# The second pass of differential attention's scores over 128 rows instead of 64, with the queries' rounded half beside zeros

## The chip, the cores and the metric

The kernel runs on one core of a Trainium2 chip. The metric is device time in microseconds (us) of one execution, as the median of several runs. The engines are TensorE (PE in the profile, with its weight loads shown apart as PEld), VectorE (DVE), ScalarE (ACT), GpSimd (POOL) and SyncE (SP, which here only issues transfers).

## The reference

One layer works on 1024 latent tokens of width 1024 and 256 context tokens. An input projection feeds two groups of heads side by side, differential attention and a gated delta rule; then come the output projection, a router with 16 experts that each take 128 tokens, and a norm. The change lies in the attention, which has four heads of two softmax halves of depth 64:

```python
def diff_attn(q, k, v, lam):
    ...
    qb = jnp.moveaxis((q * DA_D ** -0.5).reshape(B, nblk, Q_BLOCK, DA_HEADS, 2, DA_D), 1, 0)

    def block(qi):
        s = jnp.einsum('bqhid,bkhid->bhiqk', qi, k).astype(jnp.float32)
        p = jax.nn.softmax(s, axis=-1)
        a = (p[:, :, 0] - lam * p[:, :, 1]).astype(v.dtype)
        return jnp.einsum('bhqk,bkhe->bqhe', a, v)
```

The scores `s` of a block of 128 queries and one half have 1280 columns: 1024 latent and 256 context keys.

## The kernel before, in words

Float32 products of width 256 and more run as float32r passes. Each operand is split exactly into a rounded part, hi, and its rest, lo, and the product is hi·hi + lo·hi + hi·lo. Projections take three passes of depth 128 (`mm3`, L169 to L174). The scores have depth 64, so two of the three fit into one pass of depth 128. `_head` (L969) loads, for a head's half s, the tile `QS` with the queries' hi in rows 64s to 64s+63 and their lo in the other 64 rows, the tile `KH` with the keys' hi twice, and, once for both halves, `KL` with the keys' lo (half 0 in rows 0 to 63, half 1 in rows 64 to 127).

`scores` (L1023) computes one half s for a tile t of 128 queries: three column blocks of 512, 512 and 256, each with two matmuls into the same PSUM columns. The first (L1027) is `QS` by `KH` over 128 rows. The second (L1028) is the queries' hi, the 64 rows of `QS` that hold it, by the matching 64 rows of `KL`. We call these six matmuls a scores group. Then VectorE takes the negated maximum `mx` (L1030) of the 1280 columns and ScalarE the exponential `pt` with its sum (L1033). There is one PSUM buffer `sp` for the scores, so the next group waits for that exponential. `combine` joins the two halves on VectorE (L1038 to L1041), `values` transposes the result (`ptr`, L1049), copies it (`aT`, L1051) and multiplies it by the values (`po`, L1055). There are 4 heads by 8 tiles by 2 halves, so 64 groups.

In the same stage the delta rule runs beside it (`_delta`). `levels` inverts the chunks' matrices with TensorE, VectorE, ScalarE and GpSimd in turn (tiles `X`, `lm`, `LTm`, `QF`, `QTr`, `U`, `W`). `scan` walks the chunks (`psc`, `u`, `S`), `outputs` gives `O`, and `finish` (L912) norms it and multiplies it by a gate. `finish` runs twice a head, for the inner and the outer chunks: it loads the gate into the tile `gT` (L919), multiplies in place (L938), and stores `gT` to `ot_dram` (L940). For the last head it splits parts of `gT` for the output projection instead, and one part of the inner `gT` is read by `_mixed` when the first tokens of that projection are prepared.

Each engine runs its instructions in one order, which a scheduler sets when the program is built, from priorities and its own idea of durations. An engine that waits holds up whatever stands behind. `K.after` (L119) is a copy of one column on GpSimd that holds a load back.

Of the kernel before, what the change touches and what calls it, by code (L numbers as in the profile page):

```python
"""Hybrid diffusion layer: differential attention and a gated delta rule side by side, then an
expert-choice mixture of experts, on one core.

float32 products of width 256 and more run as three float32r passes over operands that are split
exactly into a rounded part and its rest (h*h + l*h + h*l); narrower ones run in float32.
"""
# [22 lines left out]
P = 128  # L29
# [9 lines left out]
H = 4  # L39
# [15 lines left out]
GT, UB, SB = 2, 4, 4  # L55
# [21 lines left out]
# the tokens that the scans finish first come first  # L77
# [31 lines left out]
class _K:  # L109
# [7 lines left out]
    def after(self, dst, src):  # L117
        """A load to dst waits until src is there."""
        self.nc.gpsimd.tensor_copy(dst, src)  # L119

    def slot(self, kind, i=None, name=None, dt=F32):
        """A buffer of the queries' or keys' size; in turn, those first that the last head's projections leave first."""
        if i is None:
            order = (0, 1) if kind == "KL" else (0, 2, 1)
            i = order[self.turn[kind] % len(order)]
            self.turn[kind] += 1
        return self.qk.tile([P, L if kind == "QS" else LT], dt, name=name or kind, tag=f"{kind}{i}")
# [4 lines left out]
    def xT(self, kt, t, n):  # L132
        """The two parts of x^T for tiles t to t + n of a group."""
# [11 lines left out]
    def rsqrt_steps(self, pool, x, n, np_=P, tag=""):  # L145
        """1/sqrt(x) for positive x [np_, n]: three Newton steps from the bit estimate."""
# [22 lines left out]
    def mm3(self, out, ah, al, bh, bl, start, stop):  # L169
        """out (+)= a.T @ b in float32, from the split operands."""  # L170
# [10 lines left out]
def _decays(K, pg, ps):  # L181
    """Decays and betas of the delta rule: [token, direction, chunk, head]."""
# [55 lines left out]
def _prep(K, pg, ps, h, kvq):  # L238
    """Norms and decays of a head's chunks, their matrices and the inverses of the 16 x 16 diagonal blocks.

    With k = r k~ (k~ before its l2 norm), c = beta r^2, N = (k~ k~^T) * decay, a chunk of 128 tokens is
        u' = (I + N c)^-1 (v / r - e^G k~ S),   S' = e^Gl S + k~^T (c e^(Gl-G) u'),
        o  = r_q (e^G q~ S + ((q~ k~^T) * decay) c u').
    Both directions share a matrix: below the diagonal the forward one, above it the backward one.
    """
# [29 lines left out]
    # queries with the decay from their chunk's start, one set per direction  # L275
# [59 lines left out]
    # a 16 x 16 block per partition, by substitution  # L335
# [11 lines left out]
    def both(t, fwd, bwd, rows, cols):  # L347
        """A part of both directions' blocks, from an element of each on."""
# [3 lines left out]
    for j in range(15):  # L352
        # forward: rows after j gain their multiple of row j; backward: rows before 15 - j
# [16 lines left out]
def _inproj(K, banks):  # L370
    """Modulation, x^T and the input projection."""
# [7 lines left out]
    with tc.tile_pool(name="p1v", bufs=1, reuse_waits="tile") as pv, \  # L379
# [21 lines left out]
        # v of the attention and a, b of the delta rule, tokens on partitions  # L401
# [15 lines left out]
    # the rest, channels on partitions  # L417
# [109 lines left out]
def _modulation(K, pe, ps, psm):  # L527
    """Shift and scale of both token sets, channels on partitions; loads the first tokens on the way."""
# [23 lines left out]
    # silu(c), silu(c_ctx)  # L552
# [10 lines left out]
    for kt in range(KT):  # L563
# [4 lines left out]
        # of the last tile the scales in float32 at once, the shifts from split parts  # L568
# [26 lines left out]
def _tokens(K, pe, ps, xts, late):  # L595
    """x^T, modulated and split."""
# [31 lines left out]
def _row_vectors(K, pool, ps):  # L628
    """Gate 1, shift 2, scale 2 and gate 2 as rows in DRAM."""
# [29 lines left out]
def _mix(K, prep, left):  # L659
    """Differential attention and the delta rule's scans, side by side."""  # L660
# [3 lines left out]
    with tc.tile_pool(name="g", bufs=1, side="right", reuse_waits="tile") as pg, \  # L664
# [29 lines left out]
        # the first tokens of the output projection, in the buffers that the attention leaves  # L694
# [13 lines left out]
def _mixed(K, t, ol, oh, lo):  # L708
    """The parts of a tile's transposed mix."""
# [12 lines left out]
def _weights(K, pw):  # L722
    """The parts of most of w_out, in the buffers that the last head's scan leaves."""
# [14 lines left out]
    # what the attention's last head leaves  # L738
# [8 lines left out]
    # what is left of them takes the parts of the last head's mix  # L747
# [4 lines left out]
def _weight(K, k, hi, lo, raw):  # L752
    """The parts of a tile of w_out, its columns scaled by the gate."""
# [10 lines left out]
def _delta(K, pg, pw, gps, ps):  # L764
    """Inverses from the 16 x 16 blocks up, T <- T - T (off-diagonal block) T, and the scans of both directions."""
# [27 lines left out]
    def levels(h, st, c0, n):  # L793
        """Doubles the blocks up to the chunk, then W and U of both directions."""
# [50 lines left out]
    def all_levels(h, st):  # L845
        """The chunks' groups in interleaved streams."""
# [4 lines left out]
    # the context's chunks come first  # L851
# [14 lines left out]
    def scan(h, st, step):  # L866
        """One chunk of each direction."""
# [27 lines left out]
    def outputs(st, step):  # L895
        """Both directions' outputs of the last two steps, chunks ascending."""
# [15 lines left out]
    def finish(h, st, inner):  # L912
        """Gated norm of the inner or the outer chunks; they go to the transposed mix."""
# [55 lines left out]
def _head(K, h):  # L969
    """Queries' parts stacked; the keys' rounded parts twice, their rests once: passes of depth 128 and 64."""  # L970
# [19 lines left out]
def _attention(K, pa, ps):  # L990
    """Latent queries over latent and context keys; the two softmax halves of a head in turn."""
# [9 lines left out]
    # the first tiles lie where the projection ends last: these are needed later than queries and keys  # L1001
# [20 lines left out]

    def scores(st, t, s):  # L1023
        sp = ps.tile([P, 1536], F32, name="sp")
        qs = st["QS"][s][:, t * P:(t + 1) * P]
        for k0, k1 in ((0, 512), (512, 1024), (1024, 1280)):
            nc.tensor.matmul(sp[:, k0:k1], qs, st["KH"][s][:, k0:k1], start=True, stop=False)  # L1027
            nc.tensor.matmul(sp[:, k0:k1], qs[64 * s:64 * s + 64], st["KL"][64 * s:64 * s + 64, k0:k1], start=False, stop=True)  # L1028
# [637 lines left out]
```

## Time and profile before

| | us |
|---|---|
| median of 3 runs | 1759.38 (1756.13 to 1769.11) |
| span of the profiled execution, first to last instruction | 1753.3 |
| PE busy | 1596.4 (91%) |
| DVE busy | 1315.1 (75%) |
| ACT busy | 916.2 (52%) |
| POOL busy | 609.9 (35%) |

The profiled execution is told by its span alone; no other time of its own is given. The median of the runs lies 6.1 us above the span. The stage in which attention and the delta rule share the core runs from about 505 to 955 us, the output projection and the router follow, and the experts take the rest from about 1130 us on. A matmul's duration in the profile includes its way through the array, so two neighbours overlap; the distance between their starts tells what one costs.

### The profile page before, as it was taken

The page shows a single profiled execution, that of the slowest core. Times are in us where ns is not written, and L with a number is a line of the kernel's source. Part 1 is how long each engine was busy: PE and PEld are TensorE (multiplying, and loading weights), DVE is VectorE, ACT ScalarE, POOL GpSimd, SP SyncE. Part 2 cuts the span into 40 slices and gives each one's busy share as a digit, 9 for nine tenths or more (in the row PEclk, how much of TensorE's full clock was granted, in tenths as well). Part 3 has the DMA queues.
Part 4 walks back from the last instruction along what each step waited for, and adds up shares of the span by engine and source line. Part 5 has one row for each costly group of instructions (what it writes and reads, how often), then busy time and mean ns, then how long its engine had stood idle before and what let it go on. Part 6 is the DMA issues. An engine that isn't in the chain of part 4 may idle for free.

```text
span 1753.3 us, 24640 instructions
## 1 busy us (share of the span) xinstructions
PE 1596.4 (91%) x8793; PEld 1303.7 (74%) x8793; DVE 1315.1 (75%) x2110; ACT 916.2 (52%) x1514; POOL 609.9 (35%) x489
## 2 busy tenths in 40 slices
PE   6999899899979999999999998399999999999990
PEld 2897678788857878787787787278888877777780
DVE  6657845678667776667777744789999989989894
ACT  6521125434324545455465232287777777777773
POOL 3013321332244662371630122434565334441012
PEclk9999899999989999999999999599999999999995
DMA  7478852443564042412212484799999999999915
GB/s 268 154 250 249 246 169 92 155 128 118 162 183 114 24 103 91 109 48 74 85 54 100 143 307 167 265 359 358 399 385 398 399 384 353 357 360 375 369 37 216
DMA packets 170846, 377.17 MB, mean 215 GB/s; under 512 B 32542, under 2 KB 82140, under 8 KB 169572
## 3 DMA queue, kind: packets, MB, share of 16 engines
q1 hardware_dynamic: 131874, 315.22, 49.5%
q0 software_dynamic: 11664, 43.52, 8.3%
q10 hardware_dynamic: 27186, 16.86, 3.8%
q8 instruction: 69, 1.13, 0.3%
q14 instruction: 53, 0.43, 0.1%
HBM read 315.60 MB, written 55.76 MB: 212 GB/s over the span
## 4 chain that ended last, share of the span: by engine, by line
PE 65%; DVE 6%; DMA 5%; POOL 3%; ACT 3%; issue 2%; SPq 0%; ACTq 0%; POOLq 0%; DVEq 0%
PE sp L1028 4%; PE pgu L172 3%; PE po L1055 3%; PE sp L1027 3%; PE pgu L173 3%; PE pgu L174 3%; PE pgv L172 3%; PE pgv L174 3%; PE pgv L173 3%; PE py L173 3%; PE py L172 3%; PE py L174 3%; PE ptr L1049 2%; PE pp L172 2%; PE pp L173 2%
## 5 line engine op out<-in xcount | busy, mean ns | idle before, releaser
L1461 DVE TENSOR_TENSOR wlo<-raw,whi 128x1024 fp32r<-128x1024 f32 x376 | 453.3, 1241 | 40.8 <-ACT whi L1460 31.6
L1460 ACT ACTIVATE whi<-raw 128x1024 fp32r<-128x1024 f32 x384 | 399.1, 1059 | 134.0 <-PE pgu L173 53.5
L1412 POOL TENSOR_SCALAR onehot<-fcst,slot 128x128 bf16<-128x128 f32 x96 | 156.9, 2027 | 42.9 <-PE pls L1415 22.5
L173 PE MATMUL pl<-XH,wl 128*128 128x512 f32 x384 | 152.9, 398 | 3.7 <-DVE wl L178 3.7
L172 PE MATMUL pl<-XH,wh 128*128 128x512 f32 x384 | 153.2, 399 | 0.9 <-DVE ab L413 0.9
L174 PE MATMUL pl<-XL,wh 128*128 128x512 f32 x384 | 153.1, 399 | 0.0
L1030 DVE TENSOR_REDUCE mx<-sp 128x1 f32<-128x1280 f32 x64 | 95.2, 1487 | 54.5 <-PE sp L1028 54.1
L1526 POOL DMA_INDIRECT acc_dram<-y,idx x15 | 36.1, 2409 | 279.6 <-DVE y L1525 265.6
L172 PE MATMUL pgu<-whi,xTh 128*128 128x512 f32 x256 | 102.1, 399 | 18.1 <-ACT hid L1505 18.1
L1033 ACT ACTIVATE pt<-sp,mx 128x1280 f32<-128x1280 f32 x64 | 84.8, 1325 | 57.4 <-DVE mx L1030 54.1
L174 PE MATMUL pgu<-wlo,xTh 128*128 128x512 f32 x256 | 101.8, 398 | 0.0
L172 PE MATMUL pgv<-whi,xTh 128*128 128x512 f32 x256 | 101.7, 397 | 0.0
L173 PE MATMUL pgu<-whi,xTl 128*128 128x512 f32 x256 | 100.8, 394 | 0.0
L174 PE MATMUL pgv<-wlo,xTh 128*128 128x512 f32 x256 | 100.4, 392 | 0.0
L1027 PE MATMUL sp<-KH,QS 128*128 128x512 f32 (+1 forms) x192 | 89.3, 465 | 12.0 <-ACT pt L1033 6.8
L173 PE MATMUL pgv<-whi,xTl 128*128 128x512 f32 x256 | 99.7, 390 | 0.0
L174 PE MATMUL py<-wlo,hTh 128*128 128x512 f32 x240 | 94.6, 394 | 0.7 <-POOL wlo L1461 0.7
L172 PE MATMUL py<-whi,hTh 128*128 128x512 f32 x240 | 93.8, 391 | 0.0
L173 PE MATMUL py<-whi,hTl 128*128 128x512 f32 x240 | 93.6, 390 | 0.0
L1028 PE MATMUL sp<-KL,QS 64*128 64x512 f32 (+1 forms) x192 | 89.6, 467 | 0.0
L1055 PE MATMUL po<-V,aT 128*128 128x128 f32 x640 | 88.7, 277 | 0.0
L172 PEld LDWEIGHTS pl<-XH,wh 128*128 128x128 f32 x384 | 73.2, 191 | 20.3 <-issue 5.2
(540 smaller groups left out, 4008.1 us busy)
## 6 DMA issues: line engine op xcount, KB each, us to landing
raw<-w_gate SPq DMA_DIRECT2D x64, 1024.0 KB
raw<-w_up SPq DMA_DIRECT2D x64, 1024.0 KB
raw<-w_down SPq DMA_DIRECT2D x64, 1024.0 KB
rwm<-w_mod POOLq DMA_DIRECT2D x32, 512.0 KB, 6.3
wr<-w_in ACTq DMA_DIRECT2D x24, 512.0 KB
wm<-w_mod SPq DMA_DIRECT2D x8, 1024.0 KB
KH<-qk_dram SPq DMA_DIRECT2D x16, 320.0 KB
xt<-x SPq DMA_DIRECT2D x8, 512.0 KB
```

Source lines behind the costliest of these rows:

```text
L172: nc.tensor.matmul(out, ah, bh, start=start, stop=False)
L173: nc.tensor.matmul(out, al, bh, start=False, stop=False)
L174: nc.tensor.matmul(out, ah, bl, start=False, stop=stop)
L1027: nc.tensor.matmul(sp[:, k0:k1], qs, st["KH"][s][:, k0:k1], start=True, stop=False)
L1028: nc.tensor.matmul(sp[:, k0:k1], qs[64 * s:64 * s + 64], st["KL"][64 * s:64 * s + 64, k0:k1], start=False, stop=True)
L1030: nc.vector.tensor_reduce(mx, sp[:, :LT], axis=AX.X, op=ALU.max, negate=True)
L1033: nc.scalar.activation(pt, sp[:, :LT], AF.Exp, bias=mx, accum_out=sm)
L1055: nc.tensor.matmul(po, aT[c], st["V"][:, c], start=c == 0, stop=c == NTT - 1)
L1412: eng.tensor_scalar(oh[:, t], iota, slot[:, t, e:e + 1], None, op0=ALU.is_equal)
L1460: nc.scalar.activation(hi, raw[:, i], AF.Copy)
L1461: eng.tensor_tensor(lo, raw[:, i], hi.bitcast(F32), ALU.subtract)
L1526: nc.gpsimd.indirect_dma_start(out=K.acc_dram, in_=y, in_offset=None, compute_op=ALU.add, out_offset=bass.IndirectOffsetOnAxis(ap=ready[e] ...
```

## The change

The queries' hi is copied beside zeros: two tiles `qz0` and `qz1` of 128 rows by 2 by 128 columns are zeroed once, and GpSimd copies, for each tile of queries, 64 rows by 128 columns for each half into one of them (`pad`), in turn. The second pass then multiplies all 128 rows of that tile by all 128 rows of `KL`; the 64 rows of the other half meet zeros. `pad` is written one tile ahead of `scores`. For the room, `gT` has one buffer instead of two. The diff also empties comments and docstrings, which changes no instruction.

```diff
-GT, UB, SB = 2, 4, 4
+GT, UB, SB = 1, 4, 4
...
+    padded = [pa.tile([P, 2, P], F32R, name=f"qz{i}") for i in range(2)]
+    for z in padded:
+        nc.gpsimd.memset(z.bitcast(F32), 0.0)
+
+    def pad(i):
+        h, t = divmod(i, NT)
+        for s in range(2):
+            rows = slice(64 * s, 64 * s + 64)
+            nc.gpsimd.tensor_copy(padded[t % 2][rows, s], heads[h]["QS"][s][rows, t * P:(t + 1) * P])
+
+    pad(0)
+
     def scores(st, t, s):
...
             nc.tensor.matmul(sp[:, k0:k1], qs, st["KH"][s][:, k0:k1], start=True, stop=False)
-            nc.tensor.matmul(sp[:, k0:k1], qs[64 * s:64 * s + 64], st["KL"][64 * s:64 * s + 64, k0:k1], start=False, stop=True)
+            nc.tensor.matmul(sp[:, k0:k1], padded[t % 2][:, s], st["KL"][:, k0:k1], start=False, stop=True)
...
     for i in range(H * NT):
         h, t = divmod(i, NT)
+        if i + 1 < H * NT:
+            pad(i + 1)
         p0 = scores(heads[h], t, 0)
```

In the changed kernel the lines behind L1022 have higher numbers: the scores' passes are L1040 and L1041, `mx` is L1043, the copies of `pad` are L1032.

The scheduler orders anew. The first place is GpSimd's order in the delta rule's first head, where `LTm`, `lm` and `W` are products of `levels`. Before:

```order
L832 TENSOR_TENSOR W_4815<-U_4814,eG_73 128x256
L805 TENSOR_TENSOR QTr_4925<-cst_65,cmp1_4860 128x512
L832 TENSOR_TENSOR W_4833<-U_4832,eG_73 128x512
L810 TENSOR_TENSOR lm_4898<-LTN_4862,cst_65 128x256
L815 TENSOR_TENSOR LTm_4930<-QTr_4925,cst_65 128x512
L810 TENSOR_TENSOR lm_4912<-LTN_4862,cst_65 128x512
```

In the changed kernel, the same products with the two copies of the seventh tile of queries (the fourth use of `qz0`):

```order
L805 TENSOR_TENSOR QTr_4925<-cst_65,cmp1_4860 128x512
L1032 COPY qz0_4954<-QS_4527 64x128
L832 TENSOR_TENSOR W_4833<-U_4832,eG_73 128x512
L815 TENSOR_TENSOR LTm_4930<-QTr_4925,cst_65 128x512
L810 TENSOR_TENSOR lm_4898<-LTN_4862,cst_65 128x256
L1032 COPY qz0_4954<-QS_4535 64x128
L810 TENSOR_TENSOR lm_4912<-LTN_4862,cst_65 128x512
```

The copies stand between the products, one at a time. They may run once the scores of the tile two before, which used the same half of `qz0`, are done.

The second place is VectorE's order at the first scores, where `fb` and `sub` belong to the last head's 16 by 16 blocks. Before, the first maximum stands among them:

```order
L1021 TENSOR_SCALAR gsub_4952<-vec_66 128x1
L1030 TENSOR_REDUCE mx_4961<-sp_4954 128x1
L359 TENSOR_TENSOR fb_4414<-fb_4414,sub_4415 80x2x5x11
L356 TENSOR_TENSOR sub_4415<-lb_4413,fb_4414 80x96
L822 TENSOR_TENSOR QF_4565<-p_d_4611,QF_4565 128x256
L359 TENSOR_TENSOR fb_4414<-fb_4414,sub_4415 80x2x4x12
```

In the changed kernel it stands behind their end and behind the attention's factor `nlam`:

```order
L364 COPY sub_4415<-fb_4414 80x256
L1015 TENSOR_TENSOR lam_4940<-lam_4940 128x128
L1016 TENSOR_REDUCE ls_4945<-lam_4940 128x2
L1018 TENSOR_TENSOR nlam_4946<-ls_4945 128x1
L1019 TENSOR_SCALAR nlam_4946<-nlam_4946 128x1
L1043 TENSOR_REDUCE mx_4969<-sp_4962 128x1
```

The first maximum has moved back by some 17 instructions. On TensorE, six matmuls of the delta rule's `p_x` and `p_d` have moved in between the first group's first and second matmul, and the rest of the first `p_d` and `p_dt` ahead of the second group.

The third place is SyncE's queue after the first head's scan, where `gT` goes to DRAM and its next gate is loaded. Before, both gates of the first head had been loaded long before (rows that stand some 40 places further up):

```order
L940 DMA ot_dram_87<-gT_5618 128x512
L919 DMA gT_6584<-gate_dram_80 128x512
L1074 DMA ot_dram_87<-oa_7004 128x512
L940 DMA ot_dram_87<-gT_5764 128x2x256
L919 DMA gT_6707<-gate_dram_80 128x2x256
```

In the changed kernel:

```order
L940 DMA ot_dram_87<-gT_5634 128x512
L919 DMA gT_5782<-gate_dram_80 128x2x256
L1087 DMA ot_dram_87<-oa_7038 128x512
L940 DMA ot_dram_87<-gT_5782 128x2x256
L919 DMA gT_6612<-gate_dram_80 128x512
```

The load of the outer gate now stands right behind the store of the inner result, whose buffer it takes.

## Rows read from the trace of the kernel before

**Rows 1.** The page: busy tenths of TensorE and the DMA engines in 40 slices.
```profile
PE   6999899899979999999999998399999999999990
...
DMA  7478852443564042412212484799999999999915
```

**Rows 2.** Windows, 505 to 955 us: length, busy PE PEld DVE ACT POOL, clock, DMA.
```profile
505.00:955.00 450.00, 433.08 (x2792) 346.38 (x2792) 326.76 (x594) 227.99 (x502) 201.63 (x183) 0.98 0.29 87
```

**Rows 3.** Timeline of one scores group: start us, us, engine, line, tile.
```profile
741.02 0.48 PE L1027 MATMUL sp<-KH,QS 128*128 128x512 f32 x1
741.42 0.18 PEld L1028 LDWEIGHTS sp<-KL,QS 64*128 64x128 f32 x1 [0.24 <-issue]
741.43 0.49 PE L1028 MATMUL sp<-KL,QS 64*128 64x512 f32 x1
741.85 0.50 PE L1027 MATMUL sp<-KH,QS 128*128 128x512 f32 x1
...
743.01 0.39 PE L1028 MATMUL sp<-KL,QS 64*128 64x256 f32 x1
743.33 2.05 PE L821 MATMUL p_d<-X,LTm 128*128 128x128 f32 x16
743.44 1.49 DVE L1030 TENSOR_REDUCE mx<-sp 128x1 f32<-128x1280 f32 x1 [2.51 <-PE sp L1028]
744.96 1.33 ACT L1033 ACTIVATE pt<-sp,mx 128x1280 f32<-128x1280 f32 x1 [3.25 <-DVE mx L1030]
```

**Rows 4.** Timelines of TensorE and its weight loads in the input projection.
```profile
423.25 0.29 PE L174 MATMUL pc<-XL,wh 128*128 128x256 f32 x1
423.37 0.28 PE L172 MATMUL pc<-XH,wh 128*128 128x256 f32 x1
...
496.09 0.48 PE L173 MATMUL pl<-XH,wl 128*128 128x512 f32 x1
496.17 0.19 PEld L174 LDWEIGHTS pl<-XL,wh 128*128 128x128 f32 x1
496.40 0.39 PE L174 MATMUL pl<-XL,wh 128*128 128x512 f32 x1
496.63 0.40 PE L172 MATMUL pl<-XH,wh 128*128 128x512 f32 x1
```

**Rows 5.** Waits, 505 to 955 us: who waited for whom, us, times, longest.
```profile
DVE mx L1030 <- PE sp L1028: 54.1, 36, 4.7
PE sp L1027 <- ACT pt L1033: 6.8, 4, 5.5
```

**Rows 6.** GpSimd by line (count, busy us, mean ns), and timelines of GpSimd and VectorE.
```profile
L345 POOL COPY fb<-cst 80x512 f32<-80x512 f32 x4 | 2.4, 609 | 0.0
L119 POOL CAST KL<-V 128x1 fp32r<-128x1 f32 x1 | 0.2, 178 | 0.0
...
701.90 0.16 DVE L163 SCALAR_TENSOR_TENSOR nt<-nt 128x4 f32<-128x4 f32 x1
...
754.07 1.26 POOL L805 TENSOR_TENSOR QF<-cst,cmp 128x512 f32<-128x512 f32 x1
754.16 1.20 DVE L163 SCALAR_TENSOR_TENSOR nt<-nt 128x4 f32<-128x4 f32 x1
```

**Rows 7.** Timelines of the SyncE queue and VectorE at gT.
```profile
699.18 0.32 SPq L940 DMA_DIRECT2D ot_dram<-gT  x1
...
714.69 0.37 SPq L940 DMA_DIRECT2D ot_dram<-gT  x1
...
972.97 0.28 DVE L178 TENSOR_TENSOR oppt<-gT,opQS 128x128 fp32r<-128x128 f32 x1
981.30 0.75 DVE L938 SCALAR_TENSOR_TENSOR gT<-p_o,convw,gT 128x512 f32<-128x512 f32 x1 [4.88 <-PE p_o L936]
```

**Rows 8.** Timeline of VectorE at the first scores.
```profile
517.59 1.48 DVE L1030 TENSOR_REDUCE mx<-sp 128x1 f32<-128x1280 f32 x1
...
522.90 0.37 DVE L364 COPY sub<-fb 80x256 f32<-80x256 f32 x1
```


## The prediction, before the result was known

> **What bounds the kernel now.** I read the page first, then the windows of the attention's stage, then the timeline of one scores group, then the waits of that stage.
>
> The slices show TensorE at nine tenths nearly everywhere, and the DMA engines near their limit only behind the 28th slice, where the experts stream their weights [rows 1]. The attention's stage lies ahead of that. In it TensorE is busy for 433.08 of 450 us, VectorE for 326.76, ScalarE for 227.99 and GpSimd for 201.63, at a granted clock of 0.98, so at the upper level, 2.4 GHz, nearly throughout [rows 2]. What follows depends on the end of this stage: the output projection takes its results, and the experts' buffers come free behind it. So a microsecond less on TensorE in the stage is a microsecond less in all, as long as TensorE stays the bound; the experts then start as a block that much earlier.
>
> What does TensorE do there? One scores group runs from 741.02 to 743.33, so it takes 2.31 us for six matmuls. Start follows start by 0.41 to 0.42 us for 512 columns and 0.32 us for 256, and the load of the 64-row weights begins at the start of its own matmul, after the weight path has idled for 0.24 us with nothing to wait for that the profile shows [rows 3]. In the input projection, where every float32r matmul has 128 rows, the next weights are loaded while the matmul before still streams: the load at 496.17 belongs to the matmul at 496.40. Starts there are 0.23 us apart for 512 columns and 0.12 us for 256, and 0.31 us for the first pair behind other work [rows 4]. Type and columns are those of the scores; what differs is that the scores alternate between 128 and 64 rows. My reading is that a weight load which changes the height of the matmul does not run ahead.
>
> The Trainium skill, TensorE: Matmul & The Clock Gate, Part 3, The mechanism, speaks against this: it says that a weight load overlaps a running matmul only where the two use different row groups. A 128-row load behind a 128-row matmul uses the same ones, so by that rule the changed pair would pay as before (the first rival). The trace of the projection disagrees, with its 0.23 us [rows 4].
>
> **The change part by part.**
>
> 1. The second pass over 128 rows. It adds no matmul and no column: 192 first and 192 second passes stay. With the prices of the projection a group takes 0.31 + 3 × 0.23 + 2 × 0.12 = 1.24 us instead of 2.31 [rows 3, 4], which is 1.07 us less. For 64 groups that is 68.5 us off TensorE. The upper bound is that the first pair also costs 0.23: 1.15 × 64 = 73.6. The lower bound is that nothing changes, 0.
>
> 2. What the shorter groups uncover. Before, 2.31 us of scores covered work on other engines. A reduction waits for scores 36 times of 64, for 54.1 us in all; in the other 28 VectorE was still busy when the scores ended [rows 5]. There an earlier end does not start the reduction earlier: 28 × 1.07 = 30 us if all of that came back as idle time on TensorE. But TensorE waited for the exponential, its next releaser in that loop, only 4 times and 6.8 us in all [rows 5], because the delta rule's matmuls and `values` stand between. The loop itself has room: from the first matmul to the end of the exponential it took 5.27 us, 741.02 to 744.96 + 1.33 [rows 3], and will take about 4.2, so 8.4 us for the two halves of a tile, while a tile has 450 / 32 = 14.1 us now and about 12.2 then. I take back a quarter of the 30, 8 us, nearer to the 6.8 that TensorE did wait, with 0 and 30 as the ends.
>
> 3. The copies on GpSimd. 64 copies of 64 by 128: the nearest rows are 0.18 us for one column and 0.61 us for 512 [rows 6]; I take 0.25, so 16 us more in a stage in which GpSimd has 248 us free [rows 2]. On time they are never near: the order places the copies of a tile once the scores two tiles earlier have left its half of `qz`, among products that need nothing later from TensorE, so a tile and a half of other work stands between copy and use. Behind a copy on GpSimd stand the products of `levels`, which start 0.25 us later. The price I see is another: a small VectorE instruction that takes 0.16 us alone took 1.20 us under a GpSimd product of 1.26 us [rows 6]. If each copy held VectorE for its own length, that would be 16 us of an engine that is not the bound. I take 2 us on the path, ends 0 and 16.
>
> 4. The front. The first reduction, at 517.59, moves behind instructions that end with the copy at 522.90 and the four of `nlam` [rows 8], so by about 5 us, and the second group with it. The zeroing of both tiles and the first four copies stand on GpSimd ahead of the first second pass, and end before that. In exchange TensorE does the delta rule's `p_d` and `p_dt` earlier, which stood behind the second group. I take 2 us lost, ends 0 and 6.
>
> 5. One `gT` buffer. In the first three heads the outer gate's load now waits for the store of the inner result and holds SyncE's queue meanwhile: behind it stand the store of `oa` and the outer store. Inner and outer store were issued 15.5 us apart, 699.18 and 714.69 [rows 7], into which one store and one load of 256 KB must fit. In the last head the outer load waits for the inner part's last reader, 972.97 + 0.28, and the outer product came at 981.30 after 4.88 us of waiting for TensorE [rows 7], 8 us for one load. I take 0; the end of the range is 5 us.
>
> The sum is 68.5 − 8 − 2 − 2 − 0 = 56.5 us, against the profiled span of 1753.3: 1696.8. The median of the runs lies 6.1 us above that span, so I expect a median of 1702.9, say 1703 us.
>
> **The rivals.**
>
> First: the pace stays. If the distance of 0.42 us came from the alternation of two weight tiles on the same accumulating columns, or from the rule cited above, 128 rows would change nothing. For it speaks that no row shows these very operands at full height; against it, that `mm3` alternates two weight tiles on the same columns too and runs at 0.23 us [rows 4]. It gives 1753.3 + 6.1 plus the small costs 2 and 2, so 1759 to 1763.
>
> Second: VectorE takes over. It is busy for 326.76 us; in a stage of 390 us that is 84% [rows 2], in one queue with two reductions and a joining of the halves for each tile. If in all of the 28 groups the gain is given back, 68.5 − 30 − 4 = 34.5 remain, and the time is 1725. For it speaks that the waits for scores, 54.1 us, are VectorE's main slack [rows 5] and are what the change eats; against it, that TensorE so seldom waited for the loop.
>
> Third, slower than before: the copies come late. GpSimd runs in order; a copy behind a run of products of 1.26 us each [rows 6] holds the second pass, with it all that stands behind on TensorE. The gain is gone where each tile waits 68.5 / 32 = 2.1 us; with 3 us, two or three products' time, it is 96 − 68.5 = 28 us slower, 1787. Against it: the copies stand almost two tiles ahead of their use. It needs GpSimd to lag by more than 20 us, where it has been the one that waits.
>
> **How the numbers follow.** The forecast, 45 to 74 us less, gets 0.74; VectorE as the bound, 20 to 45 us less, 0.15; no change 0.07; slower 0.04. The predicted time is the first case's, 1703. The range begins at 1759.4 − 73.6, so 1685, and reaches over the second rival's 1725 to 1732, the time with some 27 us gained; outside are the last two cases and the weak end of the second. A change of this kernel can be told from none at about 1%, 17.6 us. Faster by over 1% are the first two cases, 0.89; within it the first rival, 0.07; slower 0.04.
>
> **What the profile of the changed kernel would show.** Step 1: 128-row loads for L1041 that start about 0.23 us ahead of their matmul, starts 0.23 and 0.12 us apart, and a group of 1.24 us. Step 2: a stage of about 390 us with TensorE idle for some 25 us of it, and more than 6.8 us of waits for `pt`. Step 3: copies of about 0.25 us, and no wait of L1041 for GpSimd. Step 4: the first reduction near 522. Step 5: no wait of L938 for a transfer. The forecast would be wrong if the 0.23 us needed something that the projection has and the scores lack, or if the in-order queues of VectorE and ScalarE, laid out anew, made TensorE wait at places that this trace does not show.

## The result and the profile after

The changed kernel takes 1717.86 us (median of 4 runs, 1714.08 to 1718.26), against 1761.34 us for the kernel before on the same chip (4 runs, 1756.13 to 1769.11). The ratio is 0.9748, with a 95% interval from 0.9725 to 0.977: 43.5 us faster. The forecast was 1703 us, so 56.5 us faster; the range, 1685 to 1732, holds the time.

The profiled execution took 1718.15 us, with a span of 1716.4. First the page: all engines, then the reductions of the scores (busy us, mean ns, idle before and its releaser). The lines behind the edit have moved: the two passes are L1040 and L1041, the reduction L1043, the exponential L1046, the copies L1032.

```profile
PE 1528.0 (89%) x8793; PEld 1298.4 (76%) x8793; DVE 1309.4 (76%) x2110; ACT 918.6 (54%) x1514; POOL 637.6 (37%) x555
...
L1043 DVE TENSOR_REDUCE mx<-sp 128x1 f32<-128x1280 f32 x64 | 95.0, 1484 | 19.6 <-PE sp L1041 19.3
```

TensorE is busy for 1528.0 us; before it was 1596.4, so 68.4 us went, as many as step 1 named. That the two agree to 0.1 us is luck: in two kernels below, where only the reduction is shorter, TensorE's busy time moves by 7 and 8 us with the same products. A reduction now waits only 20 times for the scores, 19.3 us, where it was 36 times and 54.1 us [rows 5].

The timeline of one scores group after (start us, us, engine, line), beside [rows 3]:

```profile
699.97 0.48 PE L1040 MATMUL sp<-KH,QS 128*128 128x512 f32 x1
700.05 0.19 PEld L1041 LDWEIGHTS sp<-KL,qz 128*128 128x128 f32 x1
700.28 0.40 PE L1041 MATMUL sp<-KL,qz 128*128 128x512 f32 x1
700.29 0.19 PEld L1040 LDWEIGHTS sp<-KH,QS 128*128 128x128 f32 x1
700.52 0.39 PE L1040 MATMUL sp<-KH,QS 128*128 128x512 f32 x1
...
701.09 0.28 PE L1041 MATMUL sp<-KL,qz 128*128 128x256 f32 x1
...
701.21 0.38 PE L1062 MATMUL ptr<-ident,pt 128*128 128x128 f32 x2
```

The group runs from 699.97 to 701.21, so 1.24 us; that is also the median of the 58 groups whose six matmuls stand together, and 2.32 us was that of 60 before. The load for the second pass starts at 700.05, while the first pass is still streaming, and so do those behind it; starts lie 0.31, 0.24, 0.23 and 0.12 us apart, the steps of the input projection [rows 4]. All loads here use the same 128 rows. The rule of the Trainium skill that was cited against this (TensorE: Matmul & The Clock Gate, Part 3, The mechanism: overlap only between different row groups) does not hold in these rows.

Then why 43.5 and not 68.4? The windows from the first scores to the first reduction, to the last scores, and to the output projection's first matmul with `oh`, the part of its input that comes back from DRAM (its matmuls for the parts that never left the chip stand inside the last window) (length, then busy PE, PEld, DVE, ACT, POOL, granted clock, DMA share and GB/s). Before:

```profile
504.60:517.60 13.00, 8.55 (x30) 5.84 (x30) 12.76 (x17) 2.02 (x6) 12.74 (x14) 0.69 0.74 216
517.60:950.30 432.70, 420.21 (x2724) 336.42 (x2724) 312.15 (x575) 222.04 (x486) 189.29 (x172) 0.98 0.27 82
950.30:998.50 48.20, 44.04 (x260) 37.54 (x260) 32.57 (x96) 18.16 (x42) 0.64 (x1) 0.96 0.43 125
```

After:

```profile
507.70:526.10 18.40, 10.97 (x46) 9.28 (x46) 17.47 (x33) 2.83 (x8) 15.32 (x26) 0.62 0.50 144
526.10:906.90 380.80, 350.31 (x2712) 329.94 (x2713) 303.36 (x557) 223.68 (x488) 213.19 (x224) 0.98 0.31 93
906.90:957.20 50.30, 43.47 (x255) 36.96 (x254) 33.36 (x93) 17.70 (x40) 0.64 (x1) 0.97 0.42 125
```

The stage went from 493.9 to 449.5 us, 44.4 less. TensorE's busy time in it fell by 68.05, from 472.80 to 404.75. So its idle time rose by 23.65 us, from 21.1 to 44.75: by 3.0 at the front (4.45 to 7.43), by 18.0 between the first reduction and the last scores (12.49 to 30.49), and by 2.7 behind (4.16 to 6.83). The granted clock of the long middle part is 0.98 in both. Outside this stage the profiled executions differ by another 7.5 us (3.1 ahead of it, 4.4 behind) in the other direction; the kernel with one gT buffer alone, below, has 508.0 us ahead of its first scores and 758.7 behind the stage, as the changed kernel has 507.7 and 759.2, with an order there that hardly differs from before. So I count that as the spread of single executions; the stage's 44.4 agrees with the 43.5 of the medians.

Whom TensorE waits for in this stage (us, times, longest). Before:

```profile
PE pot L1071 <- DVE aO L1068: 2.5, 1, 2.5
PE psc L874 <- DVE S L885: 1.9, 1, 1.9
...
PE p_oo L902 <- DVE S L885: 1.2, 2, 0.7
...
PE ptr L1049 <- DVE pt L1040: 0.3, 1, 0.3
```

After, with two waits of others on top:

```profile
POOL qz L1032 <- PE sp L1041: 72.8, 28, 6.9
...
DVE mx L1043 <- PE sp L1041: 19.3, 20, 2.9
...
PE ptr L1062 <- DVE pt L1053: 7.3, 6, 2.4
...
PE sp L1040 <- ACT pt L1046: 5.6, 9, 1.7
...
PE p_dt L826 <- DVE QF L822: 4.8, 2, 4.0
PE psc L874 <- DVE S L885: 4.4, 2, 4.0
...
PE pp L172 <- ACT woh L177: 4.3, 1, 4.3
PE p_x L814 <- DVE lm L810: 3.8, 1, 3.8
...
PE p_oo L902 <- DVE S L885: 2.4, 2, 1.9
```

Without the first wait for `y`, 5.1 us in both, TensorE waited 8.3 us for VectorE before and 25.3 after, in all its rows; the larger ones stand above. The joined halves `pt`, the scan's state `S`, and the products `QF` and `lm` now come late. They don't all come late for one reason. The longest wait for `S` stands behind a reduction, which is what a crowded VectorE would look like:

```profile
643.70 1.48 DVE L1043 TENSOR_REDUCE mx<-sp 128x1 f32<-128x1280 f32 x1
...
645.74 0.58 PE L874 MATMUL psc<-S,WT 128*128 128x128 f32 x1 [4.02 <-DVE S L885]
```

But the wait for `lm` (3.8 us, ended at 512.36) and the long one for `QF` (4.0, ended at 528.29) stand at the front, among the last head's 16 by 16 blocks, where VectorE's order is a new one. And 4.3 us for `woh`, a part of the output weights, stand behind the last scores and on ScalarE. What is left for `pt` and `S` grew by 10.7 us, from 3.4 to 14.1. The exponential costs it 5.6 us, about what it did (6.8). And there is a wait that I had not named: GpSimd stands 72.8 us in 28 waits ahead of a copy, until the scores two tiles earlier have left the padded tile.

### The profile page after: what moved, and what is told of

The parts are those of the page before. It is cut to its first block, busy times and chain, and to the rows that moved or that the text cites. A ratio compares the mean times of both kernels' runs of the same rounds, so it can differ in the third digit from the quotient of the medians.

```text
span 1716.4 us, 24735 instructions
## 1 busy us (share of the span) xinstructions
PE 1528.0 (89%) x8793; PEld 1298.4 (76%) x8793; DVE 1309.4 (76%) x2110; ACT 918.6 (54%) x1514; POOL 637.6 (37%) x555
## 4 chain that ended last, share of the span: by engine, by line
PE 54%; DVE 10%; POOL 4%; ACT 3%; DMA 3%; issue 3%; SPq 1%; POOLq 0%; ACTq 0%; DVEq 0%
PE pgu L172 4%; PE pgu L173 3%; PE pgu L174 3%; PE pgv L172 3%; PE pgv L174 3%; PE pgv L173 3%; PE py L172 3%; PE py L173 3%; PE py L174 3%; PE po L1068 2%; PE ptm L1493 2%; DVE mx L1043 2%; PE sp L1040 2%; PE pl L172 1%; PE pl L174 1%
## 5 line engine op out<-in xcount | busy, mean ns | idle before, releaser
L1046 ACT ACTIVATE pt<-sp,mx 128x1280 f32<-128x1280 f32 x64 | 84.9, 1326 | 56.3 <-DVE mx L1043 55.8
L1043 DVE TENSOR_REDUCE mx<-sp 128x1 f32<-128x1280 f32 x64 | 95.0, 1484 | 19.6 <-PE sp L1041 19.3
L173 PEld LDWEIGHTS pl<-XH,wl 128*128 128x128 f32 x384 | 73.1, 190 | 21.5 <-DVE wl L178 5.4
L1040 PE MATMUL sp<-KH,QS 128*128 128x512 f32 (+1 forms) x192 | 76.2, 397 | 11.1 <-ACT pt L1046 5.6
```

What stands on the lines that cost most here:

```text
L173: nc.tensor.matmul(out, al, bh, start=False, stop=False)
L1043: nc.vector.tensor_reduce(mx, sp[:, :LT], axis=AX.X, op=ALU.max, negate=True)
L1046: nc.scalar.activation(pt, sp[:, :LT], AF.Exp, bias=mx, accum_out=sm)
```

## The experiments

Two theories stood at the start. Theory A: the height pays in full, and what is missing is cover, because VectorE and GpSimd no longer hide behind a shorter group. Theory B: the copies or the single gT buffer cost some 20 us by themselves, GpSimd's 72.8 us above all. The ratios are each to runs of the kernel before on the same chip, whose medians lie between 1759.1 and 1763.5 us.

**Everything but the height** (`e1_copies64`).

```diff
-nc.tensor.matmul(sp[:, k0:k1], padded[t % 2][:, s], st["KL"][:, k0:k1], start=False, stop=True)
+nc.tensor.matmul(sp[:, k0:k1], padded[t % 2][64 * s:64 * s + 64, s], st["KL"][64 * s:64 * s + 64, k0:k1], start=False, stop=True)
```

> The changed kernel with its two padded tiles, its copies, its zero fills and its one gT buffer, but with the second pass again over the 64 rows that hold the rounded half. So everything of the change is there except the height. Theory A (the height pays all, and the rest of the change costs little by itself; what was lost between 68.5 and the measured 43 us is cover that VectorE and GpSimd used to have): a scores group takes 2.31 us as before and the time is that of before plus the later start of the first reduction, 1759 to 1772 us, ratio 1.000 to 1.006. Theory B (the copies, through the waits for a free padded tile that stand in GpSimd's queue, or the one gT buffer, cost some 20 us by themselves): ratio 1.009 to 1.015, 1776 to 1787 us.

Measured: 1779.3 us, ratio 1.010 (1.0066 to 1.0134), so some 18 us more by the ratio and 20 by the medians, what theory B expects. The windows from the first scores to the output projection, of before and of this kernel:

```profile
504.60:998.50 493.90, 472.80 (x3013) 379.81 (x3014) 357.49 (x685) 242.23 (x534) 202.67 (x185) 0.97 0.30 89
```

```profile
508.00:1023.20 515.20, 484.81 (x3032) 389.75 (x3033) 359.03 (x689) 243.63 (x536) 227.69 (x253) 0.95 0.29 87
```

The stage is 21.3 us longer. TensorE is idle for 30.4 us of it instead of 21.1, 9.3 more. The rest is the granted clock: 0.95 of 515.2 us means 25.8 us' worth of cycles not granted, 0.97 of 493.9 means 14.8, so about 11 us, as far as two digits tell. So the rest of the change is not free, if a group takes 2.31 us as before. Where it costs, three more windows tell: the first 55.4 us of the stage before and in this kernel, and what stands behind the last scores in this kernel (before, 950.3 to 998.5, it is shown above).

```profile
504.60:560.00 55.40, 47.29 (x248) 35.70 (x249) 45.19 (x68) 17.48 (x37) 27.32 (x32) 0.84 0.58 162
```

```profile
508.00:563.40 55.40, 46.68 (x198) 35.57 (x199) 42.48 (x64) 14.41 (x29) 30.49 (x43) 0.66 0.57 164
966.30:1023.20 56.90, 46.67 (x276) 39.52 (x276) 34.98 (x101) 18.95 (x44) 2.99 (x2) 0.97 0.37 106
```

At the front the granted clock is 0.66 instead of 0.84, so 10 of the 11 us are lost in these 55 us. Behind the last scores TensorE is idle for 10.2 us instead of 4.2, so 6.1 of the 9.3 fall there; a wait of 4.3 us for `woh` is among them. Over the long stretch between, where nearly all the copies run, its idle time is 14.2 us instead of 12.5. So these 18 us stand at the two ends of the stage, and can't be read as a price that each copy asks. The changed kernel shares the wait for `woh`, but not the clock: its first 55.4 us were granted 0.84.

**The gT buffer alone** (`e4_gt1`), on the kernel before.

```diff
-GT, UB, SB = 2, 4, 4
+GT, UB, SB = 1, 4, 4
```

> The kernel before with one gT buffer in place of two and nothing else. The run with the copies and 64 rows came out at 1779 us, 20 above before, so one of its parts costs that. If it is the copies with their waits (theory B1), this kernel is within 0.3% of before: 1754 to 1764 us. If it is the missing second gT buffer (theory B2), it is 10 to 20 us slower, ratio 1.006 to 1.012.

Measured: 1761.6 us, ratio 1.0001 (0.9974 to 1.0027). The buffer costs nothing that can be measured. What remains of the 18 us of the run before it are the copies and what they bring.

**The copies without their ties** (`e14_scratch64`): made, but read by no product. The second pass takes its 64 rows from the queries' tile as before.

```diff
-nc.tensor.matmul(sp[:, k0:k1], padded[t % 2][:, s], st["KL"][:, k0:k1], start=False, stop=True)
+nc.tensor.matmul(sp[:, k0:k1], qs[64 * s:64 * s + 64], st["KL"][64 * s:64 * s + 64, k0:k1], start=False, stop=True)
```

> The changed kernel's copies and zero fills, and one gT buffer, but no product reads the copies: the second pass takes 64 rows straight from the queries' tile, as before. So GpSimd has the copies' work but none of the waits for a free padded tile, and no product waits for a copy. Against the run with the copies and 64 rows (1779 us): if the copies' own time on GpSimd and its port is what costs (theory D), 1770 to 1780 us; if it is what the copies tie together (the first group behind the levels, the waits, and the order of the work that follows from them, theory E), 1757 to 1765 us, ratio 0.997 to 1.003.

Measured: 1771.4 us, ratio 1.0058 (1.0036 to 1.0079), so 10 us: at the low end of theory D's 1770 to 1780, the copies' own time, and above theory E's 1757 to 1765. No product waits for a copy, and the copies wait for no product of the scores.

```profile
509.10:1012.80 503.70, 478.44 (x3013) 383.65 (x3013) 359.03 (x688) 242.94 (x534) 221.94 (x252) 0.96 0.30 89
```

The stage is 9.8 us longer than before: 4.2 us more of TensorE's idle time (25.3) and, at 0.96, some 5 us of clock. So about half of the 18 us is there without any wait between copies and scores. What makes it, the copies' time on GpSimd or the other order that the scheduler gave the stage with them in it, this run's time doesn't tell apart. Its windows speak for the order: behind the last scores, where no copy runs, TensorE is idle for 9.2 us instead of 4.2, more than the whole difference, again with 4.3 us for `woh`.

**The copies off GpSimd** (`e10_dma`), made by SyncE's transfers in the changed kernel.

```diff
-nc.gpsimd.tensor_copy(padded[t % 2][rows, s], heads[h]["QS"][s][rows, t * P:(t + 1) * P])
+nc.sync.dma_start(padded[t % 2].bitcast(F32)[rows, s], K.qk_dram[h, 0, 0, rows, t * P:(t + 1) * P])
```

> The changed kernel with the copies made by SyncE's DMAs from the queries' rounded half in DRAM (64 rows of 512 bytes) in place of GpSimd, whose queue then holds none of them; the waits for a free padded tile stand in SyncE's queue, ahead of the stores of the attention and the loads of the delta rule. Theory B1: GpSimd's levels come earlier and the time falls by 5 to 15 us against the changed kernel, to 1703 to 1713 us, ratio 0.967 to 0.972, unless a copy now lands late (TensorE waiting for a DMA at the second pass). Theory A: the time stays within 4 us of 1718.

Measured: 1719.5 us, ratio 0.9765 (0.9721 to 0.9809), no gain over the changed kernel. GpSimd waits for no padded tile here, and TensorE lost 1.2 us to one late transfer. Its waits for VectorE are all there (whom it waits for, us, times, longest):

```profile
PE psc L874 <- DVE S L885: 7.7, 3, 6.7
PE ptr L1062 <- DVE pt L1053: 7.2, 6, 2.4
...
PE sp L1041 <- DMA qz<-qk_dram: 1.2, 1, 1.2
```

So GpSimd's 72.8 us of standing, striking as they look, are not what the changed kernel pays for, unless the transfers cost as much at some other place, of which the waits show no more than that 1.2 us. Theory B in that form falls.

**An earlier release** (`e9_half`): the same two padded tiles, each as two of 128 columns, one for each half.

```diff
-    padded = [pa.tile([P, 2, P], F32R, name=f"qz{i}") for i in range(2)]
+    padded = [[pa.tile([P, P], F32R, name=f"qz{i}{s}") for s in range(2)] for i in range(2)]
```

> The changed kernel with each padded tile as two tiles of 128 columns, one for each half, in the same space. A copy then waits only for the products of its own half, so the first half's tile comes free half a tile of the attention earlier. If what GpSimd loses in waiting for a free padded tile is what the kernel loses (theory B1), that wait (72.8 us in 28 waits) falls to 30 to 55 us and the time by 3 to 10 us, to 1708 to 1715 us, ratio 0.969 to 0.973. If GpSimd's wait is covered and only VectorE's lag counts (theory A), the time stays at 1715 to 1720 us.

Measured: 1727.75 us, ratio 0.980 (0.976 to 0.9839), no better, and by the middle values 9 us worse, though the intervals touch.

GpSimd's wait for a padded tile, 75.8 us in 27 waits, did not fall as I had expected: the scheduler put the copies elsewhere in GpSimd's queue, and laid out the whole stage anew.

**Three padded tiles** (`e7_qz3`) **and their control** (`e8_ub3`). The third tile takes the space of one of the four buffers of the scan's `u`; the control gives up that buffer only.

```diff
-GT, UB, SB = 1, 4, 4
+GT, UB, SB = 1, 3, 4
...
-    padded = [pa.tile([P, 2, P], F32R, name=f"qz{i}") for i in range(2)]
+    padded = [pa.tile([P, 2, P], F32R, name=f"qz{i}") for i in range(3)]
```

> The changed kernel with three padded tiles in place of two, and three buffers in place of four for the scan's u, whose kilobyte the third tile takes. A copy then writes a tile whose products ended two tiles earlier. Theory B1: the wait of GpSimd for a free padded tile (72.8 us) falls under 20 us, and the time by 8 to 20 us, to 1698 to 1710 us, ratio 0.964 to 0.971. Theory A: the wait falls as well, but the time stays within 4 us of the changed kernel's 1718. If the third u buffer is missed, it shows as TensorE and VectorE waiting at the scan's u, and the time is above 1718 us.

> The changed kernel with three buffers for the scan's u in place of four and nothing else: the control of the run with three padded tiles, which came out at 1735 us, 17 above the changed kernel. There TensorE waited 15.4 us for VectorE's u. If the missing u buffer did that, this kernel is at 1730 to 1745 us, and the third padded tile gave 0 to 10; if it stays at 1715 to 1722 us, the third padded tile itself was the loss.

Measured: three tiles 1735.1 us, ratio 0.9858 (0.9813 to 0.9903); the control 1741.3 us, 0.9883 (0.9856 to 0.991). Waits in the first, then in the control:

```profile
PE psc L881 <- DVE u L876: 15.4, 3, 7.7
```

```profile
PE psc L881 <- DVE u L876: 12.1, 3, 5.9
```

The missing `u` buffer alone costs 23 us against the changed kernel, 12.1 of them as TensorE's waits for VectorE's `u`. So the loss of the first run is the buffer's. The third padded tile gives nothing that can be told from none (the intervals overlap), and GpSimd's wait is still 73.1 us; what that wait costs is not answered here.

**No copy ahead of the first scores** (`e12_front`): the first tile's second passes as before, copies from the second tile on.

```diff
+            if t == 0 and st is heads[0]:
+                nc.tensor.matmul(sp[:, k0:k1], qs[64 * s:64 * s + 64], st["KL"][64 * s:64 * s + 64, k0:k1], start=False, stop=True)
+                continue
             nc.tensor.matmul(sp[:, k0:k1], padded[t % 2][:, s], st["KL"][:, k0:k1], start=False, stop=True)
...
-    pad(0)
```

> The changed kernel with the first tile of the first head left as before (its second passes over the 64 rows, straight from the queries' tile), so that no copy stands ahead of the first scores; the copies begin with the second tile. Theory C (the front: the first group's second pass stands behind the delta rule's levels on GpSimd and TensorE, so that the first reduction comes 18.4 us after the first scores in place of 12 to 13): the first reduction comes 12 to 13 us after the first scores again, and the time falls by 4 to 7 us to 1711 to 1714 us, ratio 0.970 to 0.973 or so. Rival: what starts later there is only the scores, the levels start as before, and the rest of the attention takes it back: within 2 us of the changed kernel.

Measured: 1719.2 us, ratio 0.9762 (0.9737 to 0.9787), as the changed kernel. The windows to the first reduction and to the last scores:

```profile
504.00:516.20 12.20, 9.87 (x30) 7.06 (x30) 11.96 (x17) 2.02 (x6) 12.11 (x14) 0.50 0.76 213
516.20:905.90 389.70, 357.62 (x2732) 335.27 (x2733) 311.63 (x576) 224.81 (x490) 218.23 (x235) 0.97 0.31 91
```

The first reduction is back at 12.2 us behind the first scores, instead of 18.4. But the next window takes 389.7 us instead of 380.8, with 32.1 us of idle time instead of 30.5 and a clock of 0.97 instead of 0.98. The front's 6 us are given back later, as the rival said; theory C falls. The waits for `lm` (0.7 us) and `QF` (1.8) are short here, and the time doesn't follow.

**Fewer changes of height, no copies** (`e2_grouped`), on the kernel before.

```diff
 for k0, k1 in ((0, 512), (512, 1024), (1024, 1280)):
     nc.tensor.matmul(sp[:, k0:k1], qs, st["KH"][s][:, k0:k1], start=True, stop=False)
+for k0, k1 in ((0, 512), (512, 1024), (1024, 1280)):
     nc.tensor.matmul(sp[:, k0:k1], qs[64 * s:64 * s + 64], st["KL"][64 * s:64 * s + 64, k0:k1], start=False, stop=True)
```

> The kernel before with the six products of a scores group in another order: the three of 128 rows first, then the three of 64 rows, each still over 64 rows, no copies, no padded tiles, two gT buffers. If it is the change between the two heights that costs (six changes of some 0.18 us in a group of 2.31 us), two changes are left and a group takes about 1.24 + 2 x 0.18 = 1.6 us; 64 x 0.71 = 45 us less on TensorE, of which as large a part as in the change should arrive: ratio 0.978 to 0.988, 1720 to 1740 us. If it is the product of 64 rows itself that is slow, whatever stands before it, the group stays at 2.31 us and the ratio at 0.997 to 1.003.

Measured: 1719.05 us, ratio 0.9756 (0.9728 to 0.9785), as fast as the changed kernel and a little faster than the 1720 to 1740 us expected. One group in the timeline, and the stage's window:

```profile
694.04 0.82 PE L1027 MATMUL sp<-KH,QS 128*128 128x512 f32 x3
...
694.80 0.52 PEld L1029 LDWEIGHTS sp<-KL,QS 64*128 64x128 f32 x3 [0.25 <-issue]
694.80 0.85 PE L1029 MATMUL sp<-KL,QS 64*128 64x512 f32 x3
695.57 0.20 PEld L1050 LDWEIGHTS ptr<-ident,pt 128*128 128x128 f32 x2 [0.25 <-issue]
695.58 0.44 PE L1050 MATMUL ptr<-ident,pt 128*128 128x128 f32 x2
```

```profile
504.00:958.80 454.80, 426.21 (x3012) 372.88 (x3013) 356.44 (x685) 243.25 (x534) 202.74 (x185) 0.97 0.33 97
```

The group takes 1.54 us, 694.04 to 695.58. The three passes of 64 rows start 0.77 us ahead of what follows them, the three of 128 rows 0.76: a 64-row product is not slow. Only the first load of the other height, and the next one of 128 rows, waits for its own matmul, with 0.25 us of idle weight path each. Two changes in a group are left of six. The Trainium skill has a sentence that fits this, TensorEngine Tiling (Array Packing), Key Properties: changing the tiling mode drains TensorE. The rows agree, with some 0.18 us a change, (2.31 − 1.24) / 6, or 0.15 by this run's group, (1.54 − 1.24) / 2, if products of 64 and of 128 rows are two modes in that sentence's sense, which is my reading. TensorE's busy time in the stage is 426.2, 46.6 under before, and idle time 28.6, 7.5 above. The changed kernel's busy time is another 21.5 us lower, its idle time 16.2 us higher, and the two medians are the same.

**A shorter reduction**, in three kernels: after (`e5_mx_after`), before (`e6_mx_before`) and with grouped passes (`e15_group_mx`). The maximum is taken over the first 128 of the 1280 scores, so the exponent's offset is another number.

```diff
-nc.vector.tensor_reduce(mx, sp[:, :LT], axis=AX.X, op=ALU.max, negate=True)
+nc.vector.tensor_reduce(mx, sp[:, :P], axis=AX.X, op=ALU.max, negate=True)
```

> The changed kernel with the rows' maximum taken over the first 128 of the 1280 scores only (the exponent's offset is another number then). It takes about 64 x 1.3 = 80 us off VectorE within the attention. If the missing gain is cover (TensorE, now faster, waits for VectorE's chain: 28 us idle in the attention against 10 before), TensorE's idle time there falls to 10 to 18 us and the time by 8 to 18 us, to 1700 to 1710 us, ratio 0.966 to 0.971. If it is GpSimd, held by its waits for a padded tile, TensorE's idle time stays at 25 to 30 us and the time within 5 us of the changed kernel's 1718, ratio 0.972 to 0.978.

> The kernel before with the same cut to its maximum, over the first 128 of 1280 scores. TensorE waits for VectorE little there (10 us idle in the attention), so both theories expect little: 0 to 8 us off, ratio 0.995 to 1.000. It tells how much of the run above is not due to the change.

> The kernel with the three 128-row passes ahead of the three 64-row passes (1719 us, a group of about 1.6 us, no copies) with the maximum taken over the first 128 of 1280 scores, as in the two runs with that cut. Cutting VectorE's reduction gave nothing at a group of 2.31 us (1762 against 1759) and 17 us at 1.24 us (1701 against 1718). Theory A (VectorE's share of the loop ends up as the limit once TensorE's is short): at 1.6 us the cut gives something between, 5 to 14 us, 1705 to 1714 us, ratio 0.968 to 0.974. If the 17 us came from the other order that the scheduler made for that run, the cut gives here anything from a loss to 0 to 4 us, 1715 to 1725 us. If TensorE still is the only limit at 1.6 us, 0 to 4 us as well, with TensorE's idle time in the attention still near 21 us.

Measured: after 1700.5 us, ratio 0.9658 (0.9627 to 0.9689); before 1762.0 us, 1.0015 (0.9995 to 1.0035); grouped 1710.1 us, 0.9703 (0.9686 to 0.972). The stage's window in these three, in that order:

```profile
505.40:940.30 434.90, 397.61 (x3012) 375.62 (x3013) 286.86 (x685) 243.49 (x534) 227.96 (x251) 0.96 0.34 102
```

```profile
507.80:1000.20 492.40, 469.00 (x3012) 378.77 (x3013) 274.61 (x685) 243.71 (x534) 197.54 (x185) 0.97 0.30 90
```

```profile
511.00:949.30 438.30, 417.89 (x3013) 370.22 (x3014) 287.26 (x685) 243.10 (x534) 199.22 (x186) 0.97 0.35 102
```

The same cut takes 67 to 83 us off VectorE in the stage in each of them. With groups of 2.31 us it gives nothing, with 1.54 us it gives 9 us, with 1.24 us it gives 17. That is the series that theory A expects: the shorter the scores, the more VectorE's reduction stands in the way. But the windows don't bear it out. Here is the stretch from the first reduction to the last scores, in the same order; the second line of the kernel before is what stands behind that stretch:

```profile
523.90:894.10 370.20, 345.33 (x2710) 330.85 (x2711) 237.15 (x556) 222.46 (x484) 211.99 (x224) 0.97 0.32 97
```

```profile
519.70:935.80 416.10, 409.30 (x2691) 329.01 (x2691) 225.60 (x565) 221.60 (x482) 186.56 (x175) 0.99 0.28 84
935.80:1000.20 64.40, 50.03 (x292) 42.83 (x292) 37.35 (x106) 20.08 (x46) 0.64 (x1) 0.89 0.35 103
```

```profile
523.90:900.80 376.90, 364.22 (x2715) 324.75 (x2716) 242.73 (x573) 222.28 (x485) 186.80 (x175) 0.99 0.32 95
```

Without the cut this stretch takes 380.8 us after, 432.7 before and 395.4 grouped (515.9 to 911.3). So the cut shortens it by 10.6, 16.6 and 18.5 us, and by the least where the groups are shortest. In the kernel before the gain is lost again behind the last scores, which take 64.4 us instead of 48.2: 32 more matmuls stand there, and TensorE waits 6.0 us for `yo` and 4.3 for `woh`. Nor do TensorE's waits for VectorE go: in the changed kernel they are 21.8 us with the cut, 25.3 without, and the wait for the exponential rises from 5.6 to 13.2. The idle time of that stretch was to fall to 10 to 18 us, and is 24.9, from 30.5. The time hit theory A's range, its other mark missed. The cut also lets the scheduler order the stage anew, and an order alone can be worth as much as some of these gains: the kernel with the padded tiles in halves was 9 us slower by the middle values. So these three runs show that 17 us can be had, not that they were lost to VectorE's reduction. TensorE's idle time in the whole stage fell by 7.5 us (after) and 8.2 us (grouped); its busy time fell by 7.1 and 8.3 us as well, which I can't explain from the rows.

## Why the prediction was right, and where its sizes were not

1. The second pass over 128 rows: right. 1.24 us a group was forecast and measured. That 68.4 us came off TensorE's busy time for the 68.5 forecast is closer than that sum can be trusted. The reading that the change of height costs the time is shown by the grouped kernel, which keeps the 64 rows and has two changes in place of six. The first rival, the pace stays, is out.

2. What the shorter groups uncover: the mechanism was named, but the term was mis-sized, and it is the step that failed inside a range that held. I took back 8 us, a quarter of 30, because TensorE had waited only 6.8 us for the exponential. The idle time rose by 18.0 us between first reduction and last scores, and by 23.65 in the whole stage. The price came at other places than the loop that I looked at: TensorE's waits for VectorE went from 8.3 to 25.3 us, most of them at `pt`, `S`, `QF` and `lm`. At the exponential, where I expected more than 6.8, it waited 5.6. The prediction's last sentence had named this case, queues laid out anew that make TensorE wait at places that the old trace doesn't show. The argument that the loop of the scores has room (8.4 us of 12.2) was beside the point; VectorE's queue is shared, it is busy for 303.36 of 380.80 us now (80%, before 312.15 of 432.70, 72%), and what stands in it behind a reduction or a joining of the halves can come late, as the wait of 4.02 us for `S` shows. That this is the cause of the whole 23.65 us is not shown: 10.7 us at `pt` and `S` fit it, while `lm` and the long `QF` belong to the front's new order, `woh` to the end of the stage, and the runs with the shorter reduction don't settle it. The measured 1718 lies nearer to the second rival's 1725, VectorE takes over, than to the forecast, and 43.5 us less stands just below the band of 45 to 74 that had 0.74, in the rival's 20 to 45, which had 0.15. The range holds it because it was drawn around that rival too.

3. The copies: they were never late, as forecast; TensorE waited 0.3 us for one. A copy took 0.29 us in the median, against 0.25, and 0.39 in the mean:

```profile
L1032 POOL CAST qz<-QS 64x128 fp32r<-64x128 f32 x64 | 25.1, 393 | 83.0 <-PE sp L1041 72.8 <-DMA QS<-qk_dram 9.3
```

That GpSimd would stand 72.8 us for free tiles was not foreseen, and costs nothing that the transfers in its place could win back. But the 2 us on the path are not what the copies cost with the old pace: 10 us without ties and 18 with them, most of it at the two ends of the stage. In the changed kernel neither GpSimd's copies nor the front could be shown to cost time, so how much of the 23.65 us is theirs, and how much VectorE's alone, stays open.

4. The front: the reduction came at 526.14, against the forecast of 522. The first group's second pass went behind the delta rule's first products:

```profile
507.73 0.79 PE L1040 MATMUL sp<-KH,QS 128*128 128x512 f32 x1 [5.08 <-DVE y L510]
...
519.47 0.79 PE L1041 MATMUL sp<-KL,qz 128*128 128x512 f32 x1
...
526.14 1.49 DVE L1043 TENSOR_REDUCE mx<-sp 128x1 f32<-128x1280 f32 x1
```

The idle time there rose by 3.0 us, near the 2 forecast, but the kernel without that delay is no faster, so no run shows a price of this term.

5. One gT buffer: 0, as forecast, by its own run. In the last head the product waits for TensorE as before (4.35 us for `p_o`, at 933.28), and for no transfer.

In sum: 68.4 for 68.5, less 23.65 of idle time in the stage for the 12 that I took (8, 2 and 2). The stage was to hold some 25 us of idle time, 8 more than the 16.9 of [rows 2]; it gained 23.65.

The third rival, copies that come late, didn't come about.

## What to carry to other kernels

When a trace shows a weight load that starts only with its own matmul, compare the heights of the neighbours before counting columns: making them alike, or putting products of one height next to each other, wins the same microseconds, and the second needs no copies, no buffers and no zeros. Before adding up what is taken off TensorE, list who waits for its cover in the whole stage, not in the loop that is changed: here TensorE's new waits stood at tiles where the old trace showed next to none. When a control run changes the total, look at the windows before reading the total as a series: a gain in one stretch can be lost in the next. A long wait on an engine that isn't on the path (GpSimd's 72.8 us) is no loss until a run without it is faster.

## What the runs showed of the hardware that was not expected

The pace of 64-row products: three in a row and the change behind them take 0.77 us with 512, 512 and 256 columns (694.80 to 695.57), like three of 128 rows and the change behind those, 0.76 us (694.04 to 694.80). With the projection's steps three alone take 0.23 + 0.23 + 0.12 = 0.58 us [rows 4], which leaves 0.18 for the change. The granted clock can cost as much as the waits: the kernel with the copies and 64 rows lost some 11 us to it and 9 to idle time, and 10 of the 11 in the first 55 us of its stage, granted 0.66 against 0.84 before, so for longer at the lower level of 1.2 GHz. TensorE was idle for about as long in both stretches (8.7 and 8.1 us), so the rows don't tell why.
